# B's causal mask set inside the running product by a bank with a unit matrix, and B's query tile 3 turned by VectorE and memory

## The chip, the cores and the metric

The kernel runs on one core of a Trainium2 chip. The metric is device microseconds of one execution. Three runs of the kernel before took 762.18, 765.72 and 766.22 us; their median is 765.72 us. The profile comes from a further execution, which took 771.36 us.

A core has TensorE (PE in the profile, with its weight loads as PEld), VectorE (DVE), ScalarE (ACT), GpSimd (POOL) and SyncE (SP), which here issues all transfers between the on-chip memory SBUF and the device's memory. Matmul results land in the banks of PSUM, of which the code allots eight.

## The reference

One layer of a hybrid encoder is computed for a prompt of 1024 rows and for a sample of 32 rows with caches of 512. A normalised input is projected to queries, keys, values and gates of two groups of eight heads, A (a band with a softmax) and B (stick-breaking). Their outputs are gated, projected, normalised, and gated once more. All is float32. The change touches B:

```python
def stick_breaking(q, k, v, q_pos, k_pos):
    z = jnp.einsum('bqhd,bkhd->bhqk', q, k).astype(jnp.float32) * ATTN_SCALE
    causal = (k_pos[None, :] < q_pos[:, None])[None, None]
    log_beta = jax.nn.log_sigmoid(z)
    log_1m = jnp.where(causal, jax.nn.log_sigmoid(-z), 0.0)
    after = lax.cumsum(log_1m, axis=3, reverse=True) - log_1m
    w = jnp.where(causal, jnp.exp(log_beta + after), 0.0).astype(v.dtype)
    return jnp.einsum('bhqk,bkhd->bqhd', w, v)
```

So the weight of key k for query q is sigmoid(z) at k times the product of sigmoid(-z) over all keys between k and q, and it is zero from the diagonal on.

## The kernel before, in words

Every float32 operand is split into a rounded high part and a rest (names with h and l: `wTh`, `wTl`, `hnh`, `hnl`), and a product is two or three matmuls of these parts that add up in one bank.

The program is recorded first and put in order afterwards. `Recorder.add` notes each operation with its engine, a cost by `cost`, and what it depends on; `simulate` and `latest` run a model of the engines over the recorded operations nine times and give each a due time; in the last pass the tables `AHEAD_OF` and `AHEAD_AT` shift the due times by stage, engine and name of the result. Each engine then gets its instructions in that order (`emit`, whose line 806 is the line of nearly every instruction in the profile). PSUM banks are given out by the same model: `BANKS` says how many each kind (projections `mm`, scores `S`, turned tiles `T`, values `PV`) keeps at least, and the rest go to whichever asks first by due time.

Stage 0 normalises the input. Stages 1 to 8 run the attention of A and B in turn, a pair of heads each (A0, B0, A1, ... B3), and between it the projections of the next pair (`mm_kA`, `mm_qB` and so on), later the gates. Stages 9 to 13 are the output projection and the last gate.

One head of B has eight tiles of 128 queries. `attention` has three steps for tile i:

- `scores(i)`: two matmuls per piece of at most 512 keys into banks `SB` (a tile with over 512 keys has two pieces). VectorE adds `maskb` (-1e30 from the diagonal on) to the last 128 columns in the bank. ScalarE writes sigmoid(-z) to `w0` and sigmoid(z) to `w1`, both in the heap `be`. VectorE runs a product backwards over `w0`, from right to left, with the bank of the scores named as a second operand that the operation does not use. GpSimd multiplies `w1` by it.
- `weights_t(i)`: the weights are turned so that keys lie on partitions. Either TensorE transposes 128x128 blocks into a bank (`ptwB`), and ScalarE (`wTh`) and VectorE (`wTl`) split it from there; or, for the tiles in `ROUND`, VectorE turns 32x32 squares, SP stores them to memory (`swapB`) and loads them back as four pieces with the squares exchanged, and the split reads `be`. ROUND has tiles 4, 5 and 6 of B and 5, 6 and 7 of A.
- `values(g)`: for tiles 0 to 3 and 4 to 7 the turned weights, `wTh` and `wTl`, are multiplied with the values into a bank `PVB`.

The sample's part does the same on 544 keys, with its own mask `masks`.

Of the kernel before, what the change touches and what calls it, by code (L numbers as in the profile page):

```python
# [13 lines left out]
P = 128  # L14
# [14 lines left out]
    ('ACT', ''): -892, ('ACT', 'Kh'): 1659, ('ACT', 'L'): -618, ('ACT', 'S'): 4784,  # L29
    ('ACT', 'hnh'): -1920, ('ACT', 'junk'): -268, ('ACT', 'oT'): -448, ('ACT', 'ot'): 28,  # L30
    ('ACT', 'ple'): 2845, ('ACT', 'sg'): -1594, ('ACT', 'stq'): -1482, ('ACT', 'stv'): -538,
    ('ACT', 'v'): -1004, ('ACT', 'w'): -930, ('ACT', 'wTh'): -102, ('ACT', 'wh'): 77,
    ('ACT', 'whs'): -820, ('ACT', 'wl'): 1080, ('ACT', 'x'): 197, ('ACT', 'xS'): 296,
    ('DVE', 'Kl'): 372, ('DVE', 'L'): 463, ('DVE', 'S'): 119, ('DVE', 'Vh'): 150, ('DVE', 'diags'): 779,
    ('DVE', 'gT'): 1765, ('DVE', 'hnl'): -306, ('DVE', 'kt'): 429, ('DVE', 'newl'): -3638,
    ('DVE', 'om'): 70, ('DVE', 'ot'): -144, ('DVE', 'sgg'): 656, ('DVE', 'sq'): -493,
    ('DVE', 'uu'): 7524, ('DVE', 'w'): -311, ('DVE', 'wTl'): 124, ('DVE', 'wl'): 2196,
    ('DVE', 'wlS'): 2470, ('PE', 'Ss'): -1954, ('PE', 'g'): -930, ('PE', 'mm'): -15, ('PE', 'o'): 149,
    ('PE', 'ple'): 168, ('PE', 'ptr'): 300, ('PE', 'ptws'): 284, ('POOL', 'Qfs'): -48,
    ('POOL', 'be'): -510, ('POOL', 'bias'): -1045, ('POOL', 'g'): 1675, ('POOL', 'gT'): -1894,  # L40
    ('POOL', 'h'): 149, ('POOL', 'ms'): 607, ('POOL', 'ogg'): 81, ('POOL', 'om'): -110,
    ('POOL', 'qsS'): 1220, ('POOL', 'sgg'): 1405, ('POOL', 'w'): -451, ('POOL', 'wl'): -35,
# [3 lines left out]
}  # L46
AHEAD_AT = {
    (0, 'ACT', 'hnh'): 1395, (0, 'ACT', 'stk'): -1192, (0, 'DVE', 'hnl'): 39, (0, 'DVE', 'x'): -1474,
# [6 lines left out]
    (3, 'ACT', 'ot'): -358, (3, 'ACT', 'v'): -1119, (3, 'ACT', 'wh'): 513, (3, 'DVE', 'Kcs'): 45,  # L55
    (3, 'DVE', 'L'): -818, (3, 'DVE', 'Vh'): 157, (3, 'DVE', 'wTl'): -53, (3, 'PE', 'PVl'): 160,
    (3, 'PE', 'S'): 6, (3, 'PE', 'mm'): 89, (3, 'PE', 'ptr'): -5169, (3, 'PE', 'ptws'): 24,
    (3, 'SP', 'be'): 288, (3, 'SP', 'kl'): -604, (3, 'SP', 'swap'): 411, (3, 'SP', 'vns'): 907,
    (4, 'ACT', 'be'): -1790, (4, 'ACT', 'ot'): 139, (4, 'ACT', 'v'): 1170, (4, 'ACT', 'wTh'): 174,
    (4, 'DVE', 'Kcs'): 47, (4, 'DVE', 'Kl'): -350, (4, 'DVE', 'L'): -403, (4, 'DVE', 'Vh'): -176,  # L60
    (4, 'DVE', 'om'): 47, (4, 'DVE', 'vx'): 777, (4, 'DVE', 'w'): 522, (4, 'PE', 'PVs'): -2314,
    (4, 'PE', 'S'): 56, (4, 'PE', 'ptw'): 76, (4, 'SP', 'Kcs'): -1093, (5, 'ACT', 'be'): 42,
    (5, 'ACT', 'stk'): -951, (5, 'ACT', 'wTh'): 150, (5, 'DVE', 'om'): 77, (5, 'DVE', 'ot'): 3568,
# [4 lines left out]
    (6, 'ACT', 'stk'): 1396, (6, 'ACT', 'v'): 2717, (6, 'ACT', 'wTh'): 196, (6, 'ACT', 'wh'): 688,  # L68
    (6, 'DVE', 'S'): 9224, (6, 'DVE', 'om'): 595, (6, 'DVE', 'ot'): 412, (6, 'DVE', 'wTl'): 653,
    (6, 'PE', 'PV'): -108, (6, 'PE', 'PVl'): 183, (6, 'PE', 'S'): 51, (6, 'PE', 'mm'): 186,  # L70
    (6, 'PE', 'ptw'): 112, (6, 'SP', 'g'): 122, (6, 'SP', 'sum'): 227, (6, 'SP', 'wr'): -284,
    (7, 'ACT', 'L'): 381, (7, 'ACT', 'newh'): -334, (7, 'ACT', 'stk'): 3547, (7, 'ACT', 'wTh'): -51,
    (7, 'ACT', 'wh'): -200, (7, 'DVE', 'Vl'): -414, (7, 'DVE', 'diags'): 3279, (7, 'DVE', 'om'): 57,
# [5 lines left out]
    (8, 'ACT', 'wh'): 529, (8, 'DVE', 'S'): 51, (8, 'DVE', 'om'): 721, (8, 'DVE', 'sgg'): 329,  # L79
    (8, 'PE', 'PV'): -75, (8, 'PE', 'S'): 69, (8, 'PE', 'mm'): 310, (8, 'PE', 'ptw'): -55,  # L80
    (8, 'PE', 'ptws'): -1062, (8, 'PE', 'ptxs'): -605, (8, 'POOL', 'Qfs'): -167, (8, 'POOL', 'be'): 856,
    (8, 'POOL', 'ogg'): -399, (8, 'POOL', 'om'): 632, (8, 'POOL', 'sgg'): -2103, (8, 'POOL', 'w'): 1029,
    (8, 'POOL', 'wl'): 261, (8, 'SP', 'Kcs'): 207, (8, 'SP', 'be'): 45, (8, 'SP', 'o'): 668,
    (8, 'SP', 'og'): 832, (8, 'SP', 'ogg'): -634, (8, 'SP', 'swap'): -1099, (9, 'ACT', 'oT'): 3675,
    (9, 'ACT', 'ple'): -989, (9, 'ACT', 'wh'): 1592, (9, 'ACT', 'x'): -1192, (9, 'PE', 'ple'): -270,
# [11 lines left out]
ROUND = {"A": ((5,), (6,), (7,)), "B": ((4,), (5,), (6,))}  # L97
# [143 lines left out]
class Op:  # L241
    __slots__ = ("pieces", "eng", "what", "args", "kw", "key", "busy", "late", "ready", "left", "after", "at", "size", "shared", "table", "start", "shift", "due", "size_", "index", "users", "tiles", "old", "ldw", "kind")
# [3 lines left out]
SEM = 60  # L246
# [8 lines left out]
DVE_SET, POOL_SET = 137, 110  # L255


BANKS = {'mm': 1, 'S': 2, 'T': 1, 'PV': 1}
# [158 lines left out]
class Recorder:  # L417
# [103 lines left out]
    def cost(eng, method, args, kw, writes, reads):  # L521
# [1785 lines left out]
```

## Time and profile before

The profile lists for each engine when each instruction ran and what it waited for. A line's last part in brackets is idle time of that engine before it, and the releaser. Times are in us, the mean of one in ns.

| what | before |
|---|---|
| median of three runs | 765.72 us |
| profiled execution | 771.36 us |
| its span, first to last instruction | 769.5 us |
| instructions | 14227 |
| matmuls on TensorE | 4410 |
| ScalarE busy | 523.7 us |
| GpSimd busy | 449.6 us |
| busy share of the transfer queue | 77.7% |
| moved | 173.73 MB |

The time by stage can be told from the names of the tiles: scores of A's first head begin near 54 us, those of B's first head near 106, the last matmuls of B's values start near 552, and the output products run from 595 on.

### The profile page before, as it was taken

What the parts mean: (1) busy time and instruction counts of PE and PEld (TensorE: products, weight loads), DVE (VectorE), ACT (ScalarE), POOL (GpSimd) and SP (SyncE); (2) the same over time, 40 slices, a digit from 0 to 9 for tenths busy, and PEclk for the clock granted to TensorE, in tenths of its full rate; (3) what the DMA queues carried; (4) which work ended last, traced back from release to release, by engine and by line L of the source; (5) the groups of instructions that cost most, each with busy time, mean ns of one, the idle gap of its engine ahead of it and who ended that gap; (6) DMA issues with size and microseconds to landing.
All of it is one profiled execution on the core that took longest, in us unless ns stands there. A gap on an engine that the chain in (4) does not pass through costs nothing.

```text
span 769.5 us, 14227 instructions
## 1 busy us (share of the span) xinstructions
PE 754.2 (98%) x4410; PEld 694.2 (90%) x4410; DVE 608.4 (79%) x1067; ACT 523.7 (68%) x1122; POOL 449.6 (58%) x503
## 2 busy tenths in 40 slices
PE   8999999999999999989999999999999999999997
PEld 6999999999999999989999999989998877888786
DVE  6828879898789898868898699778444788998975
ACT  5737777887676777876778686755237867884561
POOL 5614537783365563556683455889553429699443
PEclk9999999999999999999999999999999999999999
DMA  8746879787897749887879789896679957869555
GB/s 301 240 124 180 256 183 286 199 237 230 206 230 207 203 125 251 225 229 213 250 225 257 192 226 237 253 254 199 204 246 316 293 155 229 284 213 308 203 173 190
DMA packets 202525, 173.73 MB, mean 226 GB/s; under 512 B 67009, under 2 KB 164649, under 8 KB 202450
## 3 DMA queue, kind: packets, MB, share of 16 engines
q1 hardware_dynamic: 202450, 172.83, 77.7%
q8 instruction: 35, 0.57, 0.3%
q14 instruction: 40, 0.33, 0.1%
HBM read 105.72 MB, written 58.91 MB: 214 GB/s over the span
## 4 chain that ended last, share of the span: by engine, by line
PE 87%; DMA 5%; DVE 2%; ACT 2%; SPq 2%; issue 1%; POOL 1%; ACTq 0%; DVEq 0%; POOLq 0%
PE mm_vA L806 6%; PE mm_kB L806 6%; PE mm_gB L806 6%; PE mm_qA L806 6%; PE mm_qB L806 6%; PE mm_gA L806 6%; PE PVB L806 4%; PE mm_kA L806 4%; PE SA L806 4%; PE ple L806 3%; PE mm_vB L806 3%; PE SB L806 3%; PE PVA L806 3%; PE o3P L806 3%; PE o1P L806 3%; PE g1P L806 3%
## 5 line engine op out<-in xcount | busy, mean ns | idle before, releaser
L806 POOL TENSOR_TENSOR be<-be 128x640 f32<-128x640 f32 (+8 forms) x66 | 85.2, 1296 | 55.6 <-DVE be L806 31.6
L806 DVE TENSOR_TENSOR_SCAN be<-be,SB 128x384 f32<-128x384 f32 (+5 forms) x96 | 91.3, 962 | 9.9 <-ACT be L806 6.6
L806 ACT ACTIVATE be<-SB 128x384 f32<-128x384 f32 (+5 forms) x192 | 84.5, 499 | 18.9 <-DVE be L806 7.6
L806 DVE TENSOR_TENSOR wTl<-be,wTh 128x640 fp32r<-128x640 f32 (+2 forms) x48 | 55.5, 1160 | 9.7 <-ACT wTh L806 9.2
L806 ACT ACTIVATE be<-be,statA 128x640 f32<-128x640 f32 (+3 forms) x64 | 44.4, 695 | 9.8 <-DVE statA L806 9.5
L806 DVE STREAM_TRANSPOSE be<-be 128x640 f32<-128x640 f32 (+3 forms) x56 | 47.8, 864 | 1.6 <-ACT be L806 1.4
L806 ACT CAST wTh<-be 128x640 fp32r<-128x640 f32 (+2 forms) x48 | 37.5, 782 | 10.7 <-DMA be<-swapA 7.4
L806 POOL TENSOR_TENSOR gB<-gB,gB 128x256 f32<-128x256 f32 x32 | 26.1, 839 | 29.5 <-DMA gB<-in_w_ple_gate_dram 26.2
L806 DVE CUSTOM_DVE_ANT_0 be<-SA,biasA 128x320 f32<-128x320 f32 (+3 forms) x64 | 30.0, 482 | 4.8 <-PE SA L806 4.3
L806 PE MATMUL SB<-klB,LB 128*128 128x384 f32 (+5 forms) x96 | 33.2, 346 | 0.0
L806 PE MATMUL SB<-kdB,LB 128*128 128x384 f32 (+5 forms) x96 | 33.0, 344 | 0.0
L806 POOL TENSOR_TENSOR oB<-oB,oB 128x256 f32<-128x256 f32 x32 | 26.5, 852 | 10.3 <-issue 5.3
L806 PE MATMUL ptwB<-ident,be 128*128 128x128 f32 x144 | 28.0, 275 | 3.6 <-ACT be L806 2.2
L806 PE MATMUL SA<-kdA,LA 128*128 128x320 f32 (+4 forms) x96 | 30.5, 321 | 0.0
L806 PE MATMUL SA<-klA,LA 128*128 128x320 f32 (+4 forms) x96 | 29.8, 316 | 0.0
L806 DVE TENSOR_TENSOR wTl<-ptwB,wTh 128x512 fp32r<-128x512 f32 (+3 forms) x48 | 25.3, 544 | 4.6 <-PE PVB L806 3.1
L806 POOL TENSOR_TENSOR sggB<-sggB,oggB 128x352 f32<-128x352 f32 x12 | 13.8, 1148 | 23.3 <-DVE sggB L806 23.3
L806 PE MATMUL ptwA<-ident,be 128*128 128x128 f32 x120 | 26.9, 273 | 0.0
L806 PE MATMUL PVB<-wTh,v2B 128*128 128x512 f32 (+2 forms) x96 | 26.1, 345 | 0.3 <-ACT v2B L806 0.3
L806 ACT CAST wTh<-ptwB 128x512 fp32r<-128x512 f32 (+3 forms) x48 | 21.8, 488 | 6.4 <-PE PVB L806 3.9
L806 POOL TENSOR_TENSOR klA<-stkA,kdA 64x1024 fp32r<-64x1024 f32 (+2 forms) x9 | 20.0, 2226 | 9.6 <-ACT kdA L806 9.4
L806 PE MATMUL PVA<-wTh,v2A 128*128 128x128 f32 (+3 forms) x96 | 22.4, 318 | 2.0 <-ACT wTh L806 2.0
(694 smaller groups left out, 2660.2 us busy)
## 6 DMA issues: line engine op xcount, KB each, us to landing
swapA<-be SPq DMA_DIRECT2D x24, 320.0 KB, 4.4
be<-swapA SPq DMA_DIRECT2D x96, 80.0 KB, 2.7
oB<-in_w_out_dram SPq DMA_DIRECT2D x16, 256.0 KB, 4.7
sum_dro<-oB SPq DMA_DIRECT2D x16, 256.0 KB, 3.4
gB<-in_w_ple_gate_dram SPq DMA_DIRECT2D x16, 256.0 KB, 4.2
sum_drg<-gB SPq DMA_DIRECT2D x16, 256.0 KB, 3.6
x<-in_x_prompt_dram SPq DMA_DIRECT2D x16, 256.0 KB, 4.1
h_dr<-h SPq DMA_DIRECT2D x8, 512.0 KB, 4.5
```

The lines of the kernel that those rows point to most:

```text
L806: getattr(getattr(tc.nc, o.what[0]), o.what[1])(*args, **kw)
```

## The change

Three things change.

First, the mask. A bank `unit` of PSUM is kept for all of B's heads. It is filled once by VectorE with zeros, and with the unit matrix in its last 128 columns. The addition of `maskb` to the scores is left out. In the piece that holds the diagonal the running product now starts from 0 instead of 1 and adds the unit matrix as it goes: it stays 0 until it reaches the query's own column, becomes 1 there, and is multiplied on from there. The last column of `w0` is set to 0 instead of 1. In the other pieces, and in the sample's, the unused second operand is the zero part of that bank, no longer the scores'. The sample still adds `masks`.

Second, tile 3 of each head of B joins ROUND.

Third, the planner: its prices of semaphores are given per engine (`SEM`), with a price for an operation behind another of its own engine (`AGAIN`) and an overlap at an operation's end (`EARLY`); the matmul's fixed price is 5.3 instead of 3.5 ns; VectorE and ScalarE are kept from using one bank at once; and the two tables of shifts are others throughout.

```diff
 AHEAD_OF = {
-    ('ACT', ''): -892, ('ACT', 'Kh'): 1659, ('ACT', 'L'): -618, ('ACT', 'S'): 4784,
...
+    ('ACT', 'kd'): 227, ('ACT', 'newh'): 1027, ('ACT', 'stk'): 2166, ('ACT', 'stv'): -2872,
...
-ROUND = {"A": ((5,), (6,), (7,)), "B": ((4,), (5,), (6,))}
+ROUND = {"A": ((5,), (6,), (7,)), "B": ((3,), (4,), (5,), (6,))}
...
-SEM = 60
+SEM = {"PE": 75, "ACT": 35, "DVE": 35, "POOL": 90, "SP": 27, "CTL": 0}
+AGAIN = {"PE": 0, "ACT": 33, "DVE": 60, "POOL": 83}
+EARLY = {"PE": 0, "ACT": 95, "DVE": 80, "POOL": 40}
...
-BANKS = {'mm': 1, 'S': 2, 'T': 1, 'PV': 1}
+BANKS = {'mm': 1, 'S': 2, 'T': 1, 'PV': 1, 'unit': 1}
...
+                for b in o.banks:
+                    t = max([t] + [x + SEM[e] for other, x in b.seen.items() if other != e])
...
             if ab == "B":
-                a, b, s = pieces[-1]
-                dg = s[:, b - a - P:b - a]
-                nc.vector.tensor_tensor(dg, dg, maskb, ALU.add)
-                nc.gpsimd.memset(w0[:, n:n + 1], 1.0)
+                nc.gpsimd.memset(w0[:, n:n + 1], 0.0)
...
                 for a, b, s in reversed(pieces):
-                    rev = w0[:, a + 1:b + 1][:, ::-1]
-                    nc.vector.tensor_tensor_scan(rev, rev, s, 1.0 if b == n else w0[:, b + 1:b + 2], ALU.mult, ALU.bypass)
+                    last = b == n
+                    rev = w0[:, a + 1:b + 1 - last][:, ::-1]
+                    unit = units[0][:, a + 1 - b + 512:512] if last else units[0][:, 0:b - a]
+                    nc.vector.tensor_tensor_scan(rev, rev, unit[:, ::-1], 0.0 if last else w0[:, b + 1:b + 2], ALU.mult, ALU.add if last else ALU.bypass)
...
-                    nc.vector.tensor_tensor_scan(rev, rev, s, 1.0 if b0 == NK else w0[:, b0 + 1:b0 + 2], ALU.mult, ALU.bypass)
+                    nc.vector.tensor_tensor_scan(rev, rev, units[0][:, 0:b0 - a0], 1.0 if b0 == NK else w0[:, b0 + 1:b0 + 2], ALU.mult, ALU.bypass)
...
+    units.append(psum("unit", "unit"))
+    nc.vector.memset(units[0], 0.0)
+    nc.vector.tensor_copy(units[0][:, 384:512], ident)
```

By engine the program gains and loses this: TensorE 32 transposes fewer; VectorE 64 mask additions fewer, eight turns of 128x512 more, and eight splits that read SBUF instead of a bank; ScalarE as many instructions as before, eight casts with another source; SP 40 transfers more (8 stores of 256 KB and 32 loads of 64 KB). All other instructions are the same and stand in another order. Three pieces of that order, on TensorE, SP and ScalarE, are shown where the prediction uses them.

More of the change, by code (lines that the diff above doesn't have):

```diff
@@ L28 @@
 AHEAD_OF = {
-    ('ACT', ''): -892, ('ACT', 'Kh'): 1659, ('ACT', 'L'): -618, ('ACT', 'S'): 4784,
[L30 to L40, printed above, removed]
@@ L41 @@
-    ('POOL', 'h'): 149, ('POOL', 'ms'): 607, ('POOL', 'ogg'): 81, ('POOL', 'om'): -110,
-    ('POOL', 'qsS'): 1220, ('POOL', 'sgg'): 1405, ('POOL', 'w'): -451, ('POOL', 'wl'): -35,
[3 rows of a table removed]
+    ('ACT', 'kd'): 227, ('ACT', 'newh'): 1027, ('ACT', 'stk'): 2166, ('ACT', 'stv'): -2872,
+    ('ACT', 'v'): -1022, ('ACT', 'w'): 906, ('ACT', 'wh'): 2028, ('DVE', 'Kcs'): 639, ('DVE', 'L'): 100,
+    ('DVE', 'newl'): 641, ('DVE', 'ot'): -16, ('DVE', 'stats'): -1819, ('DVE', 'v'): 258,
[5 rows of a table added]
 }
 AHEAD_AT = {
-    (0, 'ACT', 'hnh'): 1395, (0, 'ACT', 'stk'): -1192, (0, 'DVE', 'hnl'): 39, (0, 'DVE', 'x'): -1474,
[6 rows of a table removed]
@@ L55 @@
[L55 to L60, printed above, removed]
@@ L61 @@
-    (4, 'DVE', 'om'): 47, (4, 'DVE', 'vx'): 777, (4, 'DVE', 'w'): 522, (4, 'PE', 'PVs'): -2314,
-    (4, 'PE', 'S'): 56, (4, 'PE', 'ptw'): 76, (4, 'SP', 'Kcs'): -1093, (5, 'ACT', 'be'): 42,
-    (5, 'ACT', 'stk'): -951, (5, 'ACT', 'wTh'): 150, (5, 'DVE', 'om'): 77, (5, 'DVE', 'ot'): 3568,
[4 rows of a table removed]
-    (6, 'ACT', 'stk'): 1396, (6, 'ACT', 'v'): 2717, (6, 'ACT', 'wTh'): 196, (6, 'ACT', 'wh'): 688,
-    (6, 'DVE', 'S'): 9224, (6, 'DVE', 'om'): 595, (6, 'DVE', 'ot'): 412, (6, 'DVE', 'wTl'): 653,
-    (6, 'PE', 'PV'): -108, (6, 'PE', 'PVl'): 183, (6, 'PE', 'S'): 51, (6, 'PE', 'mm'): 186,
@@ L71 @@
-    (6, 'PE', 'ptw'): 112, (6, 'SP', 'g'): 122, (6, 'SP', 'sum'): 227, (6, 'SP', 'wr'): -284,
-    (7, 'ACT', 'L'): 381, (7, 'ACT', 'newh'): -334, (7, 'ACT', 'stk'): 3547, (7, 'ACT', 'wTh'): -51,
-    (7, 'ACT', 'wh'): -200, (7, 'DVE', 'Vl'): -414, (7, 'DVE', 'diags'): 3279, (7, 'DVE', 'om'): 57,
[5 rows of a table removed]
-    (8, 'ACT', 'wh'): 529, (8, 'DVE', 'S'): 51, (8, 'DVE', 'om'): 721, (8, 'DVE', 'sgg'): 329,
-    (8, 'PE', 'PV'): -75, (8, 'PE', 'S'): 69, (8, 'PE', 'mm'): 310, (8, 'PE', 'ptw'): -55,
-    (8, 'PE', 'ptws'): -1062, (8, 'PE', 'ptxs'): -605, (8, 'POOL', 'Qfs'): -167, (8, 'POOL', 'be'): 856,
@@ L82 @@
[L82 to L85, printed above, removed]
[7 rows of a table removed]
+    (0, 'PE', 'mm'): -222, (0, 'PE', 'ple'): 49, (0, 'PE', 'ptx'): -58, (0, 'SP', 'x'): -182,
+    (1, 'ACT', 'kd'): 481, (1, 'ACT', 'stv'): 3262, (1, 'ACT', 'wTh'): 1579, (1, 'DVE', 'om'): -119,
[4 rows of a table added]
@@ L93 @@
+    (3, 'DVE', 'Vh'): -3862, (3, 'DVE', 'diags'): -1181, (3, 'DVE', 'newl'): -1177,
[3 rows of a table added]
+    (4, 'DVE', 'newl'): -871, (4, 'DVE', 'ot'): 29, (4, 'DVE', 'v'): -534, (4, 'DVE', 'wTl'): 220,
[5 rows of a table added]
+    (5, 'SP', 'sum'): 1060, (6, 'ACT', 'ot'): -91, (6, 'ACT', 'v'): -540, (6, 'ACT', 'wTh'): 497,
[3 rows of a table added]
+    (7, 'ACT', 'newh'): 619, (7, 'ACT', 'ot'): -1398, (7, 'DVE', 'diags'): -313, (7, 'DVE', 'om'): -182,
[3 rows of a table added]
+    (8, 'ACT', 'wTh'): 3017, (8, 'DVE', 'Vl'): 783, (8, 'DVE', 'sgg'): -2372, (8, 'PE', 'PV'): -22,
[4 rows of a table added]
 }
-ROUND = {"A": ((5,), (6,), (7,)), "B": ((4,), (5,), (6,))}
+ROUND = {"A": ((5,), (6,), (7,)), "B": ((3,), (4,), (5,), (6,))}
@@ L241 @@
 class Op:
-    __slots__ = ("pieces", "eng", "what", "args", "kw", "key", "busy", "late", "ready", "left", "after", "at", "size", "shared", "table", "start", "shift", "due", "size_", "index", "users", "tiles", "old", "ldw", "kind")
+    __slots__ = ("pieces", "eng", "what", "args", "kw", "key", "busy", "late", "ready", "left", "after", "at", "size", "shared", "table", "start", "shift", "due", "size_", "index", "users", "tiles", "old", "ldw", "kind", "banks", "early")
 LAND = {"PE": 165, "ACT": 0, "DVE": 0, "POOL": 0, "SP": 0, "CTL": 0}
-SEM = 60
+SEM = {"PE": 75, "ACT": 35, "DVE": 35, "POOL": 90, "SP": 27, "CTL": 0}
+AGAIN = {"PE": 0, "ACT": 33, "DVE": 60, "POOL": 83}
+EARLY = {"PE": 0, "ACT": 95, "DVE": 80, "POOL": 40}
 MARGIN = 400
@@ L463, in node @@
         o.key = (self.cls if eng == "PE" else self.low, len(self.ops), len(self.ops))
-        o.shared, o.table, o.shift, o.busy, o.late, o.ldw, o.kind = False, None, 0, 0, 0, 0, None
+        o.shared, o.table, o.shift, o.busy, o.late, o.ldw, o.kind, o.banks, o.early = False, None, 0, 0, 0, 0, None, (), 0
         self.ops.append(o)
@@ L506, in add @@
             o.pieces = max(self.pieces(v) for v in args[0:2])
+        if eng in ("ACT", "DVE"):
+            o.banks = tuple({id(v.buf): v.buf for v in writes + reads if isinstance(v, View) and v.buf.psum}.values())
         o.shared = eng == "POOL"
@@ L527, in cost @@
             if method == "transpose":
-                return 3.5 + 0.4444 * args[1].shape[0], 165
-            return (3.5 + 0.4444 * args[2].free()) * (1 if args[2].buf.dtype == F32R else 4), 165
+                return 5.3 + 0.4444 * args[1].shape[0], 165
+            return (5.3 + 0.4444 * args[2].free()) * (1 if args[2].buf.dtype == F32R else 4), 165
         if eng == "ACT":
@@ L534, in cost @@
                 return 155 + 2.08 * n, 0
+            if method == "reciprocal":
+                return 155 + 6.15 * n, 0
             if method == "tensor_copy" and not psum:
@@ L616, in latest @@
             if e != "CTL":
-                free[e] = ends[o.index]
+                free[e] = ends[o.index] - o.early
             done += 1
-            sem = 0 if e == "CTL" else SEM + (MARGIN if e == "PE" else 0)
+            sem = SEM[e] + (MARGIN if e == "PE" else 0)
             for a in before[o.index]:
-                if a.eng == e and e != "SP":
-                    lag = a.busy
+                if a.eng == e and e not in ("SP", "CTL"):
+                    lag = a.busy + AGAIN[e]
                 elif a.eng == "CTL":
@@ L677, in simulate @@
             for b in line:
-                b.left, b.gone = len(b.users), 0.0
+                b.left, b.gone, b.seen = len(b.users), 0.0, {}
                 b.place.left += 1
@@ L776, in simulate @@
                     port = t + o.busy
-                free[e] = t + o.busy
+                free[e] = t + o.busy - o.early
+                for b in o.banks:
+                    b.seen[e] = t + o.busy
                 done = t + o.busy + o.late
-                last = max(last, free[e])
+                last = max(last, t + o.busy)
             if e != "CTL":
-                o.at, o.start = t, free[e] - o.busy
+                o.at, o.start = t, t
             out.append(o)
             for u in o.users:
-                if u.eng == e and e != "SP":
-                    r = t if e == "CTL" else free[e]
+                if u.eng == e and e not in ("SP", "CTL"):
+                    r = t + o.busy + AGAIN[e]
                 else:
-                    r = done + (0 if u.eng == "CTL" else SEM + (MARGIN if u.eng == "PE" else 0))
+                    r = done + SEM[u.eng] + (MARGIN if u.eng == "PE" else 0)
                 come(u, r)
@@ L1189, in stream_step @@
     sums = {}
+    units = []
     def attention(ab, p, h):
```

3 lines of the change are left out of this document (2 added, 1 removed), and 52 rows, old and new, of tables (AHEAD_AT, AHEAD_OF).

## The prediction

> **What bounds the kernel now.** I began with the page's first two parts and its chain, to see which engine sets the end.
>
> ```profile
> PE 754.2 (98%) x4410; PEld 694.2 (90%) x4410; DVE 608.4 (79%) x1067; ACT 523.7 (68%) x1122; POOL 449.6 (58%) x503
> PEclk9999999999999999999999999999999999999999
> PE 87%; DMA 5%; DVE 2%; ACT 2%; SPq 2%; issue 1%; POOL 1%; ACTq 0%; DVEq 0%; POOLq 0%
> ```
>
> TensorE is busy for 754.2 of 769.5 us at a granted clock of nine tenths or more in each slice, and 87% of the chain is its own work. So the end moves by what TensorE no longer has to do, and by what it waits. Next I listed its waits, and took the windows of the attention stages.
>
> ```profile
> PE ptwB L806 <- ACT be L806: 2.2, 1, 2.2
> PE PVA L806 <- ACT wTh L806: 2.0, 2, 1.3
> PE ple L806 <- ACT wph0True L806: 1.8, 1, 1.8
> PE ptwB L806 <- ACT stvB L806: 1.3, 1, 1.3
> PE idle L806 <- DVE newh L806: 1.3, 1, 1.3
> PE ptwsB L806 <- DVE be L806: 1.2, 1, 1.2
> PE PVB L806 <- ACT v2B L806: 0.3, 1, 0.3
> ...
> 200.00:300.00 100.00, 97.91 (x633) 94.19 (x632) 87.59 (x162) 74.40 (x164) 57.42 (x66) 1.00 0.75 194
> 300.00:400.00 100.00, 97.42 (x609) 92.90 (x608) 83.50 (x149) 75.55 (x164) 59.98 (x72) 0.98 0.84 235
> 400.00:500.00 100.00, 98.69 (x642) 95.68 (x642) 84.08 (x172) 73.77 (x167) 56.66 (x65) 1.00 0.87 231
> ```
>
> All its waits are 10.1 us. Two of them (1.8 and 1.3) are the start; 2.2 + 2.0 + 1.3 + 1.2 + 0.3 = 7.0 us lie in the attention stages. The windows show VectorE (third number) at 84 to 88% there: loaded, but not the bound. What makes TensorE wait is read from the longest of these waits, in time order.
>
> ```profile
> 335.23 4.93 SPq L806 DMA_DIRECT2D be<-swapA  x5
> 341.04 0.72 ACT L806 CAST wTh<-be 128x640 fp32r<-128x640 f32 x1 [2.81 <-DMA be<-swapA]
> 341.67 0.97 ACT L806 ACTIVATE be<-SB 128x384 f32<-128x384 f32 x2
> 342.30 0.45 PE L806 MATMUL ptwB<-ident,be 128*128 128x128 f32 x1 [2.24 <-ACT be L806]
> ```
>
> The five issues took 4.93 us, the turned tile of a head of A came late, ScalarE stood 2.81 us at its cast, the sigmoid behind that cast came late, and only when it had read its bank could TensorE go on. A tile turned through memory thus costs TensorE nothing of its own, but ScalarE stands before it and everything queued behind stands with it. The 2.0 us at PVA are the same thing, seen at the cast itself.
>
> **The transposes.** B's query tile 3 had four transposes in each of eight heads: 32 fewer. Their price is read where four stand between products of one form.
>
> ```profile
> 203.78 0.81 PE L806 MATMUL mm_qB<-hnh,wh_qB 128*128 128x352 f32 x4
> 204.43 0.60 PE L806 MATMUL ptwA<-ident,be 128*128 128x128 f32 x4
> 204.78 0.89 PE L806 MATMUL mm_qB<-hnh,wh_qB 128*128 128x352 f32 x4
> 205.50 1.46 PE L806 MATMUL mm_qB<-hnh,wl_qB 128*128 128x352 f32 x8
> 207.94 0.27 PE L806 MATMUL ptwsA<-ident,be 128*128 128x128 f32 x1
> 207.97 0.41 PE L806 MATMUL mm_qB<-hnl,wh_qB 128*128 128x352 f32 x1
> ```
>
> From start to start, four products alone take 204.43 - 203.78 = 0.65 us; four transposes and four products take 205.50 - 204.43 = 1.07 us. The difference is 0.42 us, 0.105 us for one. 32 x 0.105 = **3.4 us**. The ends: by starts alone a transpose takes 0.03 us (207.94 to 207.97), 1.0 us in all, but it pushes the product behind it; by its record's length, 0.27, it is 8.6 us, but records overlap. I take 0.105, the one that counts both. The order shows it for head 0 of B's pair 2 on TensorE, first before, then after (SB are scores, ptwB the bank of turned weights, PVA the values of A):
>
> ```order
> L806 MATMUL SB20_6_0_4659<-klB20_4056,LB20_4057 128x448
> L806 MATMUL mm_kA3_0_4680<-hnh0_198,wh_kA3_0_4400 128x352 x2
> L806 MATMUL ptwB20_3_0_4689<-ident_180,be_179 128x128 x3
> L806 MATMUL PVA21_1_4652<-wTl_175,v2A21_4136 64x384
> L806 MATMUL ptwB20_3_0_4689<-ident_180,be_179 128x128
> L806 MATMUL mm_kA3_0_4680<-hnh0_198,wh_kA3_0_4400 128x352 x2
> ```
>
> ```order
> L792 MATMUL SB20_6_0_4622<-klB20_4101,LB20_4102 128x448
> L792 MATMUL SB20_6_1_4628<-kdB20_4085,LB20_4102 128x448
> L792 MATMUL SB20_6_1_4628<-klB20_4101,LB20_4102 128x448
> L792 MATMUL mm_kA3_0_4630<-hnh0_206,wh_kA3_0_4388 128x352 x4
> L792 MATMUL mm_kA3_0_4630<-hnh0_206,wh_kA3_1_4397 128x352 x3
> L792 MATMUL PVA21_1_4670<-wTh_683,v2A21_4186 128x512
> ```
>
> The four transposes are gone and nothing has come in their place; the projection of the next keys closes the gap.
>
> **The mask, and tile 3 on the other engines.** The groups by form give both.
>
> ```profile
> L806 DVE TENSOR_TENSOR SB<-SB,maskb 128x128 f32<-128x128 f32 x64 | 17.4, 284 | 6.7 <-PE SB L806 5.7 <-ACT otB L806 0.5
> L806 DVE TENSOR_TENSOR_SCAN be<-be,SB 128x512 f32<-128x512 f32 x24 | 29.5, 1230 | 2.8 <-ACT be L806 2.3
> L806 DVE STREAM_TRANSPOSE be<-be 128x512 f32<-128x512 f32 x8 | 5.6, 699 | 0.0
> L806 DVE TENSOR_TENSOR wTl<-be,wTh 128x640 fp32r<-128x640 f32 x32 | 33.9, 1062 | 7.7 <-ACT wTh L806 7.4
> L806 DVE TENSOR_TENSOR wTl<-ptwB,wTh 128x512 fp32r<-128x512 f32 x24 | 16.2, 680 | 4.1 <-PE PVB L806 3.1 <-ACT wTh L806 1.0
> L806 ACT CAST wTh<-be 128x640 fp32r<-128x640 f32 x32 | 23.3, 728 | 9.1 <-DMA be<-swapA 7.4 <-DMA be<-swapB 1.5
> L806 ACT CAST wTh<-ptwB 128x512 fp32r<-128x512 f32 x24 | 13.9, 592 | 4.7 <-PE PVB L806 2.8 <-PE ptwB L806 1.8
> swapB<-be SPq DMA_DIRECT2D x8, 320.0 KB, 3.3
> be<-swapB SPq DMA_DIRECT2D x32, 80.0 KB, 2.8
> L806 SPq DMA_DIRECT2D be<-swapB x96: 302/432/1932, 133.3 to 532.2; - x96
> L806 SPq DMA_DIRECT2D swapB<-be x24: 319/358/823, 127.8 to 527.1; - x24
> ```
>
> VectorE loses 64 x 0.284 = 18.2 us. For tile 3 it gains eight turns of 0.699 (5.6 us) and a dearer split: 1.062 x 512/640 = 0.85 from SBUF instead of 0.68, 8 x 0.17 = 1.4 us. Net it has 11.2 us less, near 597. None of this counts in the sum, because TensorE's projections cover it; without that cover the mask would be worth 0.28 us in each score tile's chain. ScalarE's cast is even: 0.728 x 512/640 = 0.58 against 0.59.
>
> No row has a running product with an add as its second operation. From below: it is as long as now, less one column. From above: as if it took one more 0.68 us operation in each of 64 tiles, 43 us on VectorE, 640 in all and still under the span. I take no change, since columns and tensors in it stay as many. Filling the unit bank at the start (a memset and a 128-column copy) lies under TensorE's wait of 1.8 us for the first weights: nothing, at most the 0.7 of one 512-column operation.
>
> SP gets five issues more per head, 0.358 + 4 x 0.432 = 2.1 us, 16.7 us over eight heads, and 8 x 512 KB more to move. Behind each load stands whatever is next in that one queue. For the same head, before and then after, on SP (swapB20_3 is the new round trip, o_dr the results, wr and stvB weights and values for what follows):
>
> ```order
> L806 DMA sum_drg_82<-gB221_4534 128x512
> L806 DMA swapB2_148<-vxB2_4403 128x1024
> L806 DMA swapB20_5_150<-be_179 128x768
> L806 DMA swapB20_4_149<-be_179 128x640
> L806 DMA vs_drB_91<-vtB2_4485 128x32
> L806 DMA wr_kB3_0_4760<-in_w_in_dram 128x4x128
> ```
>
> ```order
> L792 DMA swapB20_3_153<-be_186 128x512
> L792 DMA o_dr2_65<-otA21_0_0_4459 64x256
> L792 DMA sum_drg_82<-gB221_4500 128x512
> L792 DMA o_dr2_65<-otA21_0_1_4561 64x256
> L792 DMA swapB20_4_154<-be_186 128x640
> L792 DMA swapB2_152<-vxB2_4263 128x1024
> L792 DMA be_186<-swapB20_3_153 32x4x128 x4
> L792 DMA wr_kB3_0_4717<-in_w_in_dram 128x4x128
> ```
>
> The values' swap and the next keys' weights now stand behind tile 3's store and loads. To price it: in the waits above, 2.2 + 2.0 = 4.2 us came through late turned tiles, of which there are 48 now (the issues list 24 stores of swapB, and A's three rounds in eight heads are 24 more). That is 0.0875 us for one; eight more make **+0.7 us**. The ends are nothing (most turned tiles delay nobody) and 8 x 2.24 = 17.9 us; I take 0.7, nearer the mean of what all 48 did.
>
> **The new order.** The tables and the planner's prices change everywhere. I count one place, where the longest wait arose: ScalarE at the same head's first scores, before and after.
>
> ```order
> L806 ACTIVATE be_179<-SB20_0_0_4446 128x128
> L806 ACTIVATE be_179<-SB20_1_0_4447 128x256
> L806 CAST wTh_665<-be_179 128x4x5x32
> L806 ACTIVATE be_179<-SB20_2_0_4522 128x384
> L806 ACTIVATE be_179<-SB20_3_0_4528 128x512
> ```
>
> ```order
> L792 ACTIVATE be_186<-SB20_0_0_4433 128x128
> L792 ACTIVATE be_186<-SB20_2_0_4489 128x384
> L792 ACTIVATE be_186<-SB20_1_0_4434 128x256
> L792 CAST wTh_683<-ptwA21_4_4_4340 128x128
> L792 CAST wTh_683<-be_186 128x4x5x32
> L792 ACTIVATE be_186<-SB20_3_0_4529 128x512
> ```
>
> The second sigmoid of tile 2, which TensorE waited for, now runs ahead of the late cast: **-2.2 us**; next in line is tile 3's, whose transposes no longer exist. Elsewhere I take the order as worth nothing; the other 4.8 us of waits in these stages may all go, or as much may be added.
>
> Sum: -3.4 - 2.2 + 0.7 = -4.9 us. The profiled execution took 771.36 us (span 769.5 and 1.9 around it) and would take 766.5. The median shown, 765.72, is 5.6 lower; with the same subtraction it becomes **760.8 us**, 0.64% less.
>
> **The rivals.** *Waits move only.* The 2.2 us return at another cast and the 0.7 come on top: 765.72 - 3.4 + 0.7 = 763.0. For it: only one wait of seven is visibly undone. Against: VectorE has 11 us less to do. If the transposes were covered after all (the change doing nothing where it counts), the time would stay at 765.7; against that speak 98% and the 0.42 us.
>
> *Late tiles, one bank fewer.* The unit matrix keeps one of the eight PSUM banks that the code allots, so TensorE waits sooner for a bank that ScalarE has still to read, and tile 3's casts add places where ScalarE stands. If each second head gets a stall like the 2.24 us above, 4 x 2.24 = 9.0 us, the time is 765.72 - 3.4 + 9.0 = 771.3, slower. It decides from 3.8 + 3.4 = 7.2 us of new waits, a little over three such stalls. Against it: score banks no longer wait for the running product, which read them before. The Trainium skill, VectorE: DVE Perf Modes, section Rules for kernel authors, advises TensorE for a 128x128 transpose where PSUM will do as its target. By that rule this change goes the wrong way and this rival wins; the trace agrees only where a transfer comes late, since TensorE's 0.42 us for four lie on the bound and VectorE's 0.70 do not.
>
> *All waits go.* With the mask out of each chain and the order redone: -3.4 - 7.0 = 755.3.
>
> **How the numbers follow.** Forecast (757.5 to 761.8): 0.38. All waits go: 0.15. Waits move or nothing happens: 0.30. Late tiles: 0.17. Half a percent, 3.8 us, is about what a measurement of this kernel can tell from no change. So faster 0.53, within it 0.30, slower 0.17. The range leaves out the lowest of the third and nearly all of the last: 754 to 769.5.
>
> **What would show it.** TensorE's matmuls 32 fewer and its busy time near 751; no maskb group; 32 stores of swapB; VectorE near 597. The waits through wTh and be should sum to no more than 5 us. It is wrong if TensorE's idle time, now 769.5 - 754.2 = 15.3 us with start and end, grows past 18, if the cast of tile 3 shows long idle time before it with score banks behind, or if SP's issues stretch as in the 4.93 us.

## The result, and the profile after

The changed kernel took **773.59 us** (median of four, 773.36 to 776.59), the kernel before beside it 764.8 (median of four, 762.18 to 766.22). The ratio is 1.0122, with a 95% interval of 1.0084 to 1.0159: slower by 8.8 us, where 760.8 was forecast. The time lies outside the range given, near the rival "late tiles, one bank fewer" with its 771.3; whether that rival's mechanism did it is what the experiments ask.

The page of the changed kernel, first its engines, then its chain:

```profile
PE 754.4 (97%) x4378; PEld 690.6 (89%) x4378; DVE 609.2 (79%) x1013; ACT 521.5 (67%) x1122; POOL 448.3 (58%) x503
...
PE 69%; DMA 12%; SPq 6%; ACT 5%; DVE 4%; issue 3%; POOL 1%; ACTq 0%; DVEq 0%; POOLq 0%
```

The 32 matmuls are gone (4410 to 4378), and TensorE is as busy as before (754.2), in a span of 774.7 instead of 769.5. Its share of the chain fell from 87 to 69%, and transfers (DMA with SP's queue) rose from 7 to 18%. TensorE's waits (in total, times, longest):

```profile
PE ptwB L792 <- ACT be L792: 5.1, 2, 3.5
PE ptwB L792 <- POOL be L792: 1.9, 2, 1.0
PE ptwA L792 <- ACT stkB L792: 1.6, 1, 1.6
PE ple L792 <- ACT wph0True L792: 1.4, 1, 1.4
PE SB L792 <- ACT be L792: 1.3, 2, 1.0
```

The kind that the prediction counted as undone, a bank whose scores ScalarE has still to read, went from 2.2 us to 5.1 + 1.3. The longest stands at the same head as before, B's pair 2, head 0. Its place in the timeline:

```profile
338.31 2.03 SPq L792 DMA_DIRECT2D be<-swapA  x4
...
343.88 0.72 ACT L792 CAST wTh<-be 128x640 fp32r<-128x640 f32 x1 [2.89 <-DMA be<-swapA]
344.51 0.59 ACT L792 ACTIVATE be<-SB 128x512 f32<-128x512 f32 x1
...
345.92 1.25 ACT L792 ACTIVATE be<-SB 128x320 f32<-128x320 f32 x3 [0.82 <-DMA swapA<-be]
...
346.99 0.45 PE L792 MATMUL ptwB<-ident,be 128*128 128x128 f32 x1 [3.53 <-ACT be L792]
```

It is the same chain: A's late turned tile, ScalarE at its cast, sigmoids of B behind it, TensorE without a bank. The cast was awaited 2.89 us instead of 2.81, and a second wait follows it: a sigmoid whose place in the heap `be` is still being read by a store to `swapA`. And the clock behind it, in windows of 2 us (PE, PEld, DVE, ACT and POOL busy; then TensorE's granted clock, the transfers' share, GB/s):

```profile
344.00:346.00 2.00, 0.00 (x0) 0.00 (x0) 1.36 (x2) 1.18 (x3) 0.00 (x0) 1.00 0.36 87
346.00:348.00 2.00, 1.01 (x4) 0.96 (x5) 1.61 (x3) 2.00 (x6) 1.07 (x1) 0.50 0.78 187
348.00:350.00 2.00, 2.00 (x9) 1.93 (x9) 1.51 (x3) 1.95 (x6) 0.46 (x2) 0.50 0.94 271
350.00:352.00 2.00, 2.00 (x8) 2.00 (x7) 1.49 (x4) 0.58 (x3) 2.00 (x3) 0.50 0.85 242
352.00:354.00 2.00, 2.00 (x11) 2.00 (x11) 1.97 (x3) 0.59 (x2) 0.25 (x1) 0.80 0.98 279
```

TensorE gets half its clock for over 6 us, and for most of this time it counts as busy. Lost are the missing halves of its busy time: 1.01 x 0.50 + 2 x (0.50 + 0.50 + 0.20) = 2.9 us. So this stall cost 3.53 + 2.9 = 6.4 us, nearly twice what its row says. In the kernel before, the profiled execution lost about as much to half clock in two places, the second at its longest wait: half of 3.42 and of 3.22 us, 3.3 us in all.

```profile
7.60:11.02 3.42, 3.42 (x9) 2.66 (x10) 1.39 (x2) 2.05 (x4) 2.05 (x4) 0.50 0.97 382
342.11:345.52 3.41, 3.22 (x12) 3.18 (x13) 2.91 (x6) 2.76 (x8) 2.06 (x3) 0.50 0.71 169
```

So the half clock does not make the difference between the two kernels.

The groups by form that the prediction priced, VectorE's first, then ScalarE's, then SP's issues of B's stores:

```profile
L792 DVE TENSOR_TENSOR wTl<-be,wTh 128x640 fp32r<-128x640 f32 x32 | 37.9, 1186 | 12.4 <-ACT wTh L792 11.2 <-DMA o_dr<-otA 1.1
...
L792 DVE TENSOR_TENSOR_SCAN be<-be,unit 128x511 f32<-128x511 f32 x16 | 19.2, 1199 | 0.8 <-ACT be L792 0.7
...
L792 DVE TENSOR_TENSOR wTl<-be,wTh 128x512 fp32r<-128x512 f32 x8 | 6.1, 757 | 5.2 <-ACT wTh L792 5.1
```

```profile
L792 ACT CAST wTh<-be 128x640 fp32r<-128x640 f32 x32 | 23.4, 732 | 15.3 <-DMA be<-swapA 14.6 <-DMA be<-swapB 0.6
...
L792 ACT CAST wTh<-be 128x512 fp32r<-128x512 f32 x8 | 5.0, 623 | 4.4 <-DMA be<-swapB 4.3
```

```profile
L792 SPq DMA_DIRECT2D swapB<-be x32: 319/387/1347, 117.5 to 534.0; - x32
```

The running product with an add is as long as it was (1199 ns for 511 columns, 1230 for 512 before). ScalarE's idle time before the casts of 640 columns went from 9.1 to 15.3 us, nearly all of it for A's tiles; tile 3's own casts (the form of 512) add 4.4.

**Where 5.1 us of it went.** From the first matmul's start to the last one's, the profiled execution grew from 762.9 to 768.0 us. I took the starts of all matmuls of a trace. Each interval has the median interval of its width in the kernel before (161 ns for 352 columns, 231 for 512, 29 for a transpose); what goes beyond it by more than 100 ns I call waiting, the rest work. Waiting so includes short waits that the profile counts as busy, and the half clock.

| | work | waiting |
|---|---|---|
| before | 746.9 | 16.1 |
| changed | 743.6 | 24.4 |

TensorE works 3.3 us less, as forecast (3.4), and waits 8.3 us more. This splits the difference of two executions, both slower than their kernel's median (by 6.6 us before, by 3.0 changed); the medians lie 8.8 us apart. The question is what the waiting belongs to: the new mask with its bank, tile 3 through memory, or the order that new prices and tables give. The theories: **order** (prices and tables), **late tiles** (tile 3), **bank** (the mask's unit bank leaves seven).

### The profile page after: what moved, and what is told of

Read it like the earlier page. It is cut to its first block, busy times and chain, and to the rows that moved or that the text cites. A ratio compares the mean times of both kernels' runs of the same rounds, so it can differ in the third digit from the quotient of the medians.

```text
span 774.7 us, 14140 instructions
## 1 busy us (share of the span) xinstructions
PE 754.4 (97%) x4378; PEld 690.6 (89%) x4378; DVE 609.2 (79%) x1013; ACT 521.5 (67%) x1122; POOL 448.3 (58%) x503
## 4 chain that ended last, share of the span: by engine, by line
PE 69%; DMA 12%; SPq 6%; ACT 5%; DVE 4%; issue 3%; POOL 1%; ACTq 0%; DVEq 0%; POOLq 0%
SPq L792 6%; PE mm_gB L792 6%; PE mm_qA L792 6%; PE mm_kA L792 5%; PE mm_vA L792 4%; PE mm_kB L792 3%; PE ple L792 3%; PE PVB L792 3%; PE mm_qB L792 3%; PE SB L792 3%; PE g0P L792 3%; PE g2P L792 2%; PE g1P L792 2%; PE o0P L792 2%; PE o3P L792 2%
## 5 line engine op out<-in xcount | busy, mean ns | idle before, releaser
L792 POOL TENSOR_TENSOR be<-be 128x1024 f32<-128x1024 f32 (+8 forms) x66 | 87.6, 1336 | 38.6 <-ACT be L792 13.7
L792 DVE TENSOR_TENSOR_SCAN be<-be,unit 128x383 f32<-128x383 f32 (+9 forms) x100 | 92.3, 944 | 8.0 <-ACT be L792 5.9
L792 DVE TENSOR_TENSOR wTl<-be,wTh 128x640 fp32r<-128x640 f32 (+3 forms) x56 | 64.2, 1153 | 21.5 <-ACT wTh L792 20.3
L792 ACT CAST wTh<-be 128x640 fp32r<-128x640 f32 (+3 forms) x56 | 42.4, 762 | 26.4 <-DMA be<-swapA 14.6
L792 ACT ACTIVATE be<-be,statA 128x640 f32<-128x640 f32 (+4 forms) x64 | 44.5, 696 | 17.2 <-DVE statA L792 16.5
L792 POOL TENSOR_TENSOR klA<-stkA,kdA 64x1024 fp32r<-64x1024 f32 (+2 forms) x9 | 21.5, 2386 | 16.7 <-ACT kdA L792 16.0
L792 PE MATMUL SA<-kdA,LA 128*128 128x320 f32 (+2 forms) x96 | 30.1, 316 | 0.0
L792 PE MATMUL SA<-klA,LA 128*128 128x320 f32 (+2 forms) x96 | 29.8, 313 | 0.0
L792 PE MATMUL PVB<-wTh,v2B 128*128 128x512 f32 (+2 forms) x96 | 25.9, 340 | 0.1
L792 DVE TENSOR_TENSOR wTl<-ptwA,wTh 128x128 fp32r<-128x128 f32 (+3 forms) x48 | 22.0, 478 | 4.0 <-ACT wTh L792 3.8
L792 POOL TENSOR_TENSOR h<-h,x 128x512 f32<-128x512 f32 (+1 forms) x18 | 23.4, 1317 | 2.6 <-DVE h L792 2.6
L792 PE MATMUL PVB<-wTl,v2B 128*64 128x128 f32 (+2 forms) x96 | 24.2, 360 | 0.0
```

The source lines that it names most:

```text
L792: getattr(getattr(tc.nc, o.what[0]), o.what[1])(*args, **kw)
```

## The experiments

The runs came in five groups; the kernel before took 764.8 to 767.7 us beside them.

**One part undone.** First the changed kernel with tile 3 back on TensorE:

```diff
-ROUND = {"A": ((5,), (6,), (7,)), "B": ((3,), (4,), (5,), (6,))}
+ROUND = {"A": ((5,), (6,), (7,)), "B": ((4,), (5,), (6,))}
```

> The changed kernel with B's query tile 3 turned by TensorE again (32 transposes back, 40 issues fewer on SP); mask, unit bank, prices and tables as changed. Theory order (the tables and prices lose the time): about 773.6 + 3.4 = 777. Theory late tiles (tile 3's turn through memory loses it): 773.6 - 12.2 + 3.4 = about 765, and the waits of TensorE through ScalarE's turned weights fall from some 7 to under 5 us. Theory bank (seven banks instead of eight): 777, as for order.

It took 778.59 us: late tiles falls here, since the time rises by 5.0. Then the mask back, with tile 3 as changed:

```diff
-BANKS = {'mm': 1, 'S': 2, 'T': 1, 'PV': 1, 'unit': 1}
+BANKS = {'mm': 1, 'S': 2, 'T': 1, 'PV': 1}
...
+                a, b, s = pieces[-1]
+                dg = s[:, b - a - P:b - a]
+                nc.vector.tensor_tensor(dg, dg, maskb, ALU.add)
...
-                    nc.vector.tensor_tensor_scan(rev, rev, unit[:, ::-1], 0.0 if last else w0[:, b + 1:b + 2], ALU.mult, ALU.add if last else ALU.bypass)
+                    nc.vector.tensor_tensor_scan(rev, rev, s, 1.0 if b == n else w0[:, b + 1:b + 2], ALU.mult, ALU.bypass)
```

> The changed kernel with the mask as it was (64 additions on VectorE, the running product reads the score banks, eight banks free for work); tile 3, prices and tables as changed. Theory order: about 773.6, more by what the 64 additions show (0.28 us each in a chain, at most 18). Theory late tiles: 773.6 too. Theory bank: 773.6 - 12.2 = about 761.4.

785.35 us: bank falls here too. Both edits together leave the old computation with the changed prices and tables:

> Both parts undone, the mask and tile 3: only the changed prices and tables are left. Theory order: 773.6 + 3.4 = about 777. Theory late tiles: about 765. Theory bank: about 765.

**786.79 us**, 1.0278 (1.0245 to 1.031) of the kernel before, which computes the same. The order alone costs 21.6 us, and both parts win some of it back. The mirror image, both parts in the prices and tables of before:

> The kernel before with both parts, the new mask and tile 3 through memory, but the prices and tables of before. Theory order: 764.8 - 3.4 + 0.7 = about 762. Theory late tiles: 764.8 - 3.4 + 12.2 = about 773.6. Theory bank: about 773.6. As the tables of before were not made for these parts, up to 5 us more would tell little.

798.43 us. So a set of tables on a computation it was not made for tells little, and the tables had to go.

**Without tables.** The two tables were emptied, for each computation and each set of prices:

```diff
-AHEAD_OF = {
-    ('ACT', ''): -892, ('ACT', 'Kh'): 1659, ('ACT', 'L'): -618, ('ACT', 'S'): 4784,
...
+AHEAD_OF = {}
+AHEAD_AT = {}
```

> The kernel before with its two tables of shifts empty: the same computation, ordered by the planner's due times alone. All theories: slower than 765.2, by what its tables are worth; from the two misfits seen (21.6 us for a table on a computation it was not made for, 33.2 for the other) I expect 785 to 800. It is the base of the next three.

> The same with both parts (mask from the unit bank, tile 3 through memory), prices of before, tables empty. Theory order: the parts gain where no table fits either side, 3 to 10 us less than the plain old kernel. Theory late tiles, and theory bank: 8 us or more above it.

> The old computation with the planner's changed prices, tables empty. If the prices are what loses: 8 us or more above the plain old kernel. If only the tables: within 4 us of it.

> The changed kernel with its tables empty (both parts, changed prices). Theory order: 3 to 10 us under the old computation with these prices, and its tables are worth some 10 us less than those of before are worth to the kernel before. Theory late tiles or bank: 8 us or more above the old computation with these prices.

768.29, 780.53, 789.83 and 774.02 us. The tables of before are worth 2.3 us to the kernel before (1.0029, 1.0016 to 1.0042), not the 20 and more that I expected, and those of the changed kernel 0.4 to it. What moves the time is the order that the prices give: with the changed ones the old computation is 21.5 us slower and the new one 6.5 faster. "Prices" stands here for all of the planner's change but the tables: semaphores, `AGAIN`, `EARLY`, the matmul's 5.3, the rule for banks, and two small ones that the list of the change leaves out (a price for the reciprocal, and `DVE_SET` 139 for 137). They were not taken apart. By the old prices the parts lose 12.2, by the changed ones they gain 15.8.

**The late casts moved.** Does the stall at B's pair 2 go when the cast lets the sigmoids pass? The order was left as planned, and single instructions of ScalarE handed on behind the next ones:

```diff
-        ops = self.order()
+        ops = hand_on(self.order(), [('cast', 17, 0, 3), ('cast', 31, 2, 1), ('cast', 31, 0, 3)])
...
+    for x, reach in todo:
+        group = [x] + [o for o in x.users if what_follows(x) and o.eng in ("DVE", "POOL")]
...
+        acts = [o for o in ops[at[id(x)] + 1:stop] if o.eng == "ACT"][:reach]
+        if acts:
+            for o in group:
+                ops.remove(o)
+            i = ops.index(acts[-1]) + 1
+            ops[i:i] = group
```

> The changed kernel as it is, but at its two places where a late turned tile of A holds ScalarE (span times 225.4 and 343.9 us), the cast of that tile and its split stand behind the next three sigmoids of B, and at the second place one sigmoid that waits for its tile stands behind one that does not. Nothing else moves. Theory late tiles in ScalarE's order: the stalls of TensorE there (1.6 and 3.5 us) go, and with them the half clock behind the second, 7 us at 0.50 to 0.80 that cost 3.4: 773.6 - 8.5 = about 765. Rival, the bank or the tile is late for another reason, so the stall stays in another name: within 2 us of 773.6.

775.72 us (772.5 to 777.74): no gain. Its timeline at the second place:

```profile
340.67 1.09 ACT L792 ACTIVATE be<-SB 128x512 f32<-128x512 f32 x2
...
343.55 0.44 ACT L792 ACTIVATE be<-SB 128x320 f32<-128x320 f32 x1 [1.80 <-DMA swapA<-be]
343.88 0.72 ACT L792 CAST wTh<-be 128x640 fp32r<-128x640 f32 x1
344.50 0.44 ACT L792 ACTIVATE be<-SB 128x320 f32<-128x320 f32 x1
...
345.38 0.41 PE L792 MATMUL ptwB<-ident,be 128*128 128x128 f32 x2 [1.66 <-issue]
```

The cast no longer waits, and the two sigmoids run over 3 us earlier. But ScalarE then stands at the next sigmoid, whose place in `be` a store of A's turned weights still reads, and TensorE stops one transpose later, for 1.66 us (the row names no releaser). This execution is the fastest of its four, and no half clock follows the stall in it; the other three took 775.07 to 777.74 us. So what is saved at this place does not show in the median, and what takes it back is not shown. A tile turned through memory holds twice: with its cast, and with the room it keeps until the store has landed. With two more places (the list begins `('cast', 5, 0, 9), ('vt', 2, 0, 1)`):

> The same, and two more places: the late cast at 109.9 us behind one sigmoid and the table load, and at 185.8 us the copy of late turned values behind the copy of the keys whose bank TensorE waits for (1.6 us). Theory late tiles in ScalarE's order: 1.5 to 2.6 us less than the one with two places. Rival: no less.

774.22 us, as the changed kernel within its spread, though 1.5 us under the one with two places. And the same at the kernel before, for the step that the prediction counted as -2.2 (`hand_on(self.order(), [('cast', 27, 0, 3)])`):

> The kernel before, with the late cast at 341.0 us behind three more operations of ScalarE, among them the second sigmoid of tile 2 that TensorE waits for there: what the prediction counted as -2.2. Theory late tiles in ScalarE's order: 2.2 and the half clock behind it (1.7) go, 766 - 4 = about 762. Rival, the wait moves to the next sigmoid: 764 to 766.

767.72 us, 1.0014 (0.9998 to 1.003) of the kernel before. The rows of its trace, ScalarE's and then TensorE's:

```profile
339.13 0.73 ACT L806 CAST wTh<-be 128x640 fp32r<-128x640 f32 x1
...
342.08 0.60 ACT L806 ACTIVATE be<-SB 128x512 f32<-128x512 f32 x1 [1.83 <-DVE be L806]
...
342.82 0.52 PE L806 MATMUL ptwB<-ident,be 128*128 128x128 f32 x3 [1.66 <-ACT be L806]
```

The cast stands behind the sigmoids and waits for nothing; ScalarE now stands at the next sigmoid, whose place in `be` VectorE has still to give up, TensorE waits 1.66 instead of 2.24, and the time gains nothing.

**How much an order is worth by itself.** One price of the planner was changed by 4 ns, the computation untouched (`-SEM = 60`, `+SEM = 64`, tables empty):

> The kernel before with its tables empty and one price of the planner changed by 4 ns (a semaphore, 60 to 64), the computation untouched. If an order's worth follows its prices smoothly: 768.3, within 2 us. If each order is a new draw of waits: anywhere from 766 to 790, and then neither part can be charged with a few us that two orders differ by.

776.47 us against 768.29: 8.2 us for 4 ns in a model. That is nearly as much as the whole result, so a part can only be judged over several orders. The next runs fill a square: each part in the two orders of the old prices, tables empty.

> The kernel before, tables empty, with the mask's part alone (unit bank, running product from it, seven banks left). Theory order: anywhere from 765 to 790, and over the square no part's mean is more than 5 us from nothing. Theory bank: 8 us or more above the old computation's 768.3, and in the other order above 776.5, in both.

> The same with the semaphore's price 64. Theory order: anywhere from 765 to 790. Theory bank: 784 or more.

> The kernel before, tables empty, with tile 3 through memory alone. TensorE's own work 3 us less in any order. Theory order: the time anywhere from 763 to 787. Theory late tiles: 773 or more, with stalls through the turned weights' casts that the old computation does not have.

> Both parts, tables empty, semaphore 64 (with 60 it took 780.5). Theory order: anywhere from 765 to 790, so as likely under 776.5, the old computation's in that order, as over. Theories bank and late tiles: 784 or more.

> Tile 3 through memory alone, tables empty, semaphore 64; the old computation took 776.5 in that order. Theory late tiles: 3 to 15 us above it, 780 to 792. Theory order: as likely under 776.5 as over.

The last one is the changed prices, tables empty, tile 3 back on TensorE:

> The changed kernel with its tables empty and tile 3 turned by TensorE. Theory late tiles: 3 to 15 us under the 774.0 of the changed kernel with empty tables, 759 to 771. Theory order: anywhere from 765 to 790, since the same prices gave 789.8 for the old computation.

All medians, in us (the changed kernel and the kernel before are the corners of the first and the last row; a dash was not run):

| prices, tables | old computation | mask alone | tile 3 alone | both |
|---|---|---|---|---|
| before's, before's | 764.8 | - | - | 798.4 |
| before's, empty | 768.3 | 777.4 | 783.5 | 780.5 |
| before's with 64, empty | 776.5 | 775.2 | 785.9 | 784.7 |
| changed, empty | 789.8 | 779.8 | - | 774.0 |
| changed, changed | 786.8 | 778.6 | 785.4 | 773.6 |

**Tile 3 through memory.** In the two rows of the old prices with empty tables it costs 15.2, 3.1, 9.4 and 9.5 us: 9.3 in the mean, in all four pairs a loss. Under the changed prices it gains 5.8, 1.4 and 5.0. **The mask** costs 9.1 and gains 1.3, 3.0 and 1.2 under the old prices (+0.9 in the mean); under the changed ones it gains 10.0, 8.2 and 11.8. Four of these differences are not clear of noise, as the runs of the two versions overlap: the mask's 1.3, 3.0 and 1.2, and tile 3's 1.4. Some pairs also come from different groups.

Of the theories, late tiles held in the four runs with tile 3 under the old prices and empty tables (780.5 to 785.9), and fell under the changed ones (779.8 with tile 3 back, where 759 to 771 was expected). Bank held with both parts (780.5, 784.7) and for the mask alone at 60 (777.4); it fell for the mask alone at 64 (775.2, where 784 or more was expected) and under the changed prices. Order expected no part's mean over 5 us from nothing, and tile 3's 9.3 is. None of the three holds in all rows. Work and waiting for tile 3's pairs, by the count of starts above, in us and from one execution of each version:

```
                      work: TensorE -> memory   waiting: TensorE -> memory
old prices            745.3 -> 742.1            14.0 -> 34.5
  with the mask       745.3 -> 741.4            23.1 -> 30.0
old prices, 64        745.3 -> 743.1            22.9 -> 34.6
  with the mask       745.6 -> 742.4            22.1 -> 34.8
changed, empty, mask  744.7 -> 742.8            27.0 -> 23.2
changed, tables       746.4 -> 743.1            31.8 -> 33.2
  with the mask       746.1 -> 743.6            22.9 -> 24.4
```

In all seven pairs TensorE works less, by 1.9 to 3.9 us, 2.9 in the mean. The waiting rises by 6.9 to 20.5 under the old prices; under the changed ones it changes by -3.8, +1.4 and +1.5. The latter is not because the turned tiles come in time there. ScalarE's waits for them, in the changed kernel and then with tile 3 back:

```profile
ACT wTh L792 <- DMA be<-swapA: 14.6, 12, 2.9
ACT wTh L792 <- DMA be<-swapB: 11.3, 6, 4.9
```

```profile
ACT wTh L792 <- DMA be<-swapA: 4.6, 2, 3.8
ACT wTh L792 <- DMA be<-swapB: 2.5, 1, 2.5
```

25.9 us against 7.1, and yet the first is the faster kernel: these waits count only where a bank or a product stands behind them.

## Why the prediction was wrong, by its steps

**The transposes (-3.4): right.** TensorE's work fell by 3.3 us here and by 2.9 over seven pairs.

**The longest wait undone by the order (-2.2): wrong, and shown twice.** The sigmoid of tile 2 did run ahead, but the wait came back at the next operation, 3.53 us in place of 2.24. In the kernel before, the same edit by itself gained nothing. I had treated the wait as if one instruction owned it. At this head the casts, the sigmoids' places in `be` and the banks are all late together, so who goes first hardly matters. The prediction's own sentence, "next in line is tile 3's, whose transposes no longer exist", named the successor and then let it off: the sigmoid of tile 3 still reads a bank.

**The rest of the order at nothing: the step that failed most.** On the old computation the changed prices and tables cost 21.6 us, and by this path the result is 765.2 + 21.6 (order) - 1.4 (tile 3) - 11.8 (mask) = 773.6. By the other path, in before's prices with empty tables, the parts cost 12.2 together (768.3 to 780.5) and the prices then gain 6.5 (to 774.0). Which share of the 8.8 us belongs to a part depends on the path, so no single split is right. Settled is that the loss is waiting, not work, and that the same computation takes 764.8 to 789.8 us (the old) or 773.6 to 798.4 (the new) by its order. The range should have carried that; the prediction allowed 4.8 us either way.

**Eight more turned tiles (+0.7): mis-sized under the old prices,** where less work (-2.9) and the waiting (6.9 to 20.5 us more) make +9.3. Pricing them at the mean of the 48 already there failed; that those had found the places that had slack is a guess. Under the changed prices the waiting rises by 1.5 at most, near the 0.7. The rule cited in the prediction (the Trainium skill, VectorE: DVE Perf Modes, section Rules for kernel authors: a 128x128 transpose to TensorE where PSUM will do) agrees with the old prices' four pairs, and not with the changed prices' three, of which two are clear of noise.

**The mask at nothing on the path:** +0.9 in the mean under the old prices, but 8.2 to 11.8 gained under the changed ones. The running product's price was right. VectorE was to fall to 597 and stayed at 609.2: the mask's group is gone, the additions for tile 3 came as forecast (6.1 us for the eight splits, where 6.8 was meant), and other splits from SBUF grew, 1062 to 1186 ns for 640 columns, 4.0 us in 32. The other 8 us are spread over many small groups, and why they grew is not shown.

**The rival "late tiles, one bank fewer"** came near the time, 771.3 for 773.6; as far as the runs show, that was luck. Its chain is the one in the longest stall, but that the bank or tile 3 caused it is not shown: with the changed prices, undoing either made the kernel slower. A unit matrix held outside PSUM, which would test the bank alone, was not tried.

**What was to show it.** Matmuls, the mask's group and 32 stores came as said. The waits through turned weights and sigmoids were 5.1 + 1.3 + 0.3 = 6.7 us, over the 5 named, and TensorE's idle time 774.7 - 754.4 = 20.3, over the 18 that were to mean "wrong".

Why the changed prices suit the new computation and not the old stays open. Only one set of them was run, and none a few ns beside it; since 4 ns moved an order of the old prices by 8.2 us, that it is the prices and not the draw of one order is not shown either. No version here beats the kernel before; the nearest are its own order without tables (768.3) and with one cast moved (767.7).

## What to carry to other kernels

In a kernel at 98% of one engine whose order comes from a planner, a part's own work could be forecast (3.4 us for a mean of 2.9, 1.9 to 3.9 in single pairs), and the waits of the new order could not: change one price by a few ns first and see how far the time moves, and give the range that width. Judge a part over several orders, not in one. And before counting a wait as undone, ask what the waiting engine meets next: the stall is gone only when every late thing at that place is.

## What was not expected of the hardware

TensorE's granted clock fell to 0.50 after a stall and stayed there for 3.41 or 6.83 us. It did so after 2.24 us of waiting in the kernel before and after 3.53 in the changed one. With tile 3 back on TensorE, 1.74 us were enough, as its row shows:

```profile
341.33 0.49 PE L792 MATMUL SB<-kdB,LB 128*128 128x384 f32 x1 [1.74 <-ACT stvB L792]
```

But in the changed kernel without tables a wait of 3.11 us was not followed by it:

```profile
354.74 1.40 PE L753 MATMUL mm_kA<-hnh,wh_kA 128*128 128x352 f32 x7 [3.11 <-ACT stvB L753]
```

So length alone does not decide. The traces record when the granted clock changes, and in each of the twenty the changes lie whole steps of 3.41 us apart. Here are windows cut at these steps, for the kernel with tile 3 back and then for the changed one without tables:

```profile
338.18:341.59 3.41, 1.67 (x11) 1.42 (x11) 0.62 (x2) 1.11 (x3) 1.34 (x1) 1.00 0.47 113
341.59:345.00 3.41, 3.41 (x13) 3.41 (x13) 2.18 (x4) 3.38 (x8) 0.10 (x1) 0.50 0.55 140
345.00:348.41 3.41, 3.41 (x23) 3.28 (x22) 3.21 (x4) 2.75 (x7) 2.54 (x5) 1.00 0.77 185
```

```profile
349.60:353.02 3.42, 2.03 (x13) 1.61 (x11) 1.08 (x2) 1.00 (x2) 2.87 (x4) 1.00 0.66 177
353.02:356.43 3.41, 1.69 (x11) 1.65 (x11) 3.35 (x5) 2.80 (x6) 1.82 (x2) 1.00 0.86 299
356.43:359.84 3.41, 3.41 (x21) 3.19 (x20) 3.41 (x5) 1.90 (x5) 3.41 (x4) 1.00 0.70 220
```

The wait of 1.74 us lay in one step, in which TensorE was busy for 1.67 us, and the next step had half clock. The wait of 3.11 us was cut by a border of two steps, in which TensorE was busy for 2.03 and 1.69 us. Over the twenty traces, up to the last matmul, all 22 steps at full clock in which TensorE was busy for less than 0.45 of the time are followed by half clock. Of the 17 with a share from 0.45 to 0.53, nine are, and of the 4404 above that, four. So in this case, but for those four, it is the busy share of one step that decides, with its border near one half.

The Trainium skill, TensorE: Matmul & The Clock Gate, section "Part 1: The HAM clock gate (the "warmup" mystery)", says that the clock is halved after at least one idle window of about 3.4 us, and that the window runs freely. The traces agree with the halving, with the window's length and with its running freely. They do not agree that it must be idle: about half idle was enough, 1.74 us of it here, and the measurement decides.
